# State space chunks of a hybrid decoder step: two products moved from GpSimd to VectorE, and the inter-chunk part added where the diagonal part is read from PSUM

## The chip, the cores and the metric

The kernel runs on one core of one Trainium2 chip. The metric is the device time of one execution in microseconds; lower is better. Engines are named as the profile names them: PE is TensorE (PEld its weight loads), DVE is VectorE, ACT is ScalarE, POOL is GpSimd, SP is SyncE, which issues most of the DMAs.

## The reference

One inference step of a hybrid decoder layer on 1024 prompt tokens and 8 x 4 sample tokens, width 1024, all in float32. The part that the change touches is the Mamba-2 mixer (16 heads of 64, two B/C groups, state 128), computed exactly in chunks of 128 tokens:

```python
CB = jnp.einsum('bclgn,bcsgn->bcgls', Cm, Bm)
y_diag = jnp.einsum('bcgls,bcgkls,bcsgkp->bclgkp', CB, Lmat, xdt)
states = jnp.einsum('bcsgn,bcsgk,bcsgkp->bcgkpn', Bm, decay_st, xdt)
def step(h, inp):
    st, dec = inp
    return h * dec[..., None, None] + st, h
y_off = jnp.einsum('bclgn,bcgkpn,bclgk->bclgkp', Cm, starts, jnp.exp(acs))
y = y_diag + y_off + xs * d_skip.astype(F32).reshape(G, K)[..., None]
```

Lmat is the lower triangle of exp of differences of the cumulative decays `acs`; `starts` are the states before each chunk. Beside it in the same layer stand a pooling mixer, a gated linear recurrence (LRU), an output projection, cross attention and a feed-forward part.

## The kernel before

Channels lie on partitions, tokens along the free dimension. A projection takes a strip of weights of 128 columns, in two halves of reduced precision (`whi`, `wlo`, made from `wraw` by ACT L123 and DVE L124), and streams the 1056 tokens in three pieces of 352 (`unit`, L147): 24 matmuls to a piece, into one of three PSUM tiles `mm`. For the x, B and C channels (`xbc_proj`, L516) ACT copies the piece out twice (L500, L501), DVE applies the convolution in three steps (L503, and L509 for the sample tokens), ACT takes the tanh (L530) and DVE finishes the SiLU (L531).

The state space chunks are a generator (`ssd`, L708) that is stepped from within the projections: `unit` calls `tick` twice, and a step that says `yield 4` goes on four ticks, that is two pieces, later. Each of the two groups g (eight heads each) goes through eight chunks. A chunk has two steps.

- `first` (L550): ACT turns the rows of decays that a DMA has spread over all partitions (tiles `seg`, two per chunk, L547) into exponentials, `ea` (L556) and `seg` (L558, L559). PE makes the scores C·B (`pcb`) and transposes B and x (L562, L569). DVE masks the scores into `cbm` (L564) and makes `xdt` (L571, from PSUM) and `xdd` (L573, from `xdt`). POOL multiplies both `seg` tiles by `cbm` (L575).
- `second` (L578): PE computes the inter-chunk part `po` (L584), the new state `pst` from `xdd` (L588) and the diagonal part `pdg` from `seg` and `xdt` (L596), one behind the other. DVE makes `yt` = `po` times `ea` (L585). POOL decays the state `hs` (L586, tile h in the profile) and DVE adds `pst` to it (L590). DVE adds x times the skip weight and `pdg` (L600, four times per chunk), and POOL adds `yt` to that (L602, four times).

Group 0 begins beside the projections of group 1's channels and runs on beside `pool` (L822), group 1 beside `pool` and `lru` (L760). While group 1 runs, the sample's state space steps (`ssd_sample`, L614) run too: POOL decays a state (L696), DVE adds to it (L700), ACT's queue issues its store (L701), and SP loads the next state into the same tile (L680). In `pool`, window sums go to and fro between DVE and POOL (L800, L812), ACT writes the result `ya` (L819). In `lru`, PE needs the convolved tile `xc` (L503) for its gates `pr` and `pi` (L722, L723).

The order of PE's and SP's instructions is that of the program text (L64). That of ACT, DVE and POOL is set by a scheduler in this part of the program. Every engine goes through its own list in order, and a DMA that ACT issues holds up what stands behind it on ACT until its data is there.

Of the kernel before, what the change touches and what calls it, by code (L numbers as in the profile page):

```python
# [12 lines left out]
OP = mybir.AluOpType  # L13
PSUM = bass.MemoryType.PSUM

P = 128
# [43 lines left out]
def hybrid_step(ctx, tc, xT, memT, consts_d, masks_d, wbd_d, poolw_d, spool_d, w_kv, w_xbc, w_dt, w_lg, w_pool, w_z, h0_d,  # L60
                w_out1, w_out2, w_q, kc_d, vc_d, w_o, w_gu, w_down,
                yT, ktT, vN, smallo, pssd, sssd):
    nc = tc.nc
# [11 lines left out]
    def nm(s):  # L75
        cnt[0] += 1
        return f"{s}{cnt[0]}"
# [30 lines left out]
    def smps(shape=(P, 512), name="sm"):  # L108
        return ps.tile(list(shape), F32, tag="sm", name=nm(name), bufs=sm_bufs)
# [58 lines left out]
    def cc(name, i=None, n=1):  # L168
        a, b = COFF[name]
        return cst[:, a:b] if i is None else cst[:, a + i:a + i + n]  # L170
# [247 lines left out]
    cd = sd.tile([P, 256], F32, name="cd")  # L418
# [95 lines left out]
    xbc = [None] * 12  # L514
# [18 lines left out]
    r8 = lambda t: t.rearrange("p (h q) -> p h q", h=8)  # L533

    def ssd_prompt(g):

        Bt, Ct = xbc[8 + g], xbc[10 + g]
        hs = sd.tile([P, 512], F32, tag=f"h{g}", name=nm("h"), bufs=1)
        tk = lambda c: slice(c * P, (c + 1) * P)
        h0 = lambda c: c * 16 + g * 8  # L540
        bc8 = lambda t, c: t[:, h0(c):h0(c) + 8][:, :, None].to_broadcast([P, 8, 64])

        def load(c):

            segs = [sd.tile([P, 4, P], F32, tag="seg", name=nm("seg"), bufs=4) for _ in range(2)]
            for q in range(2):
                nc.sync.dma_start(segs[q], acs_dram[None, h0(c) + 4 * q:h0(c) + 4 * q + 4, :].to_broadcast([P, 4, P]))  # L547
            return segs

        def first(c, segs):  # L550
            ea = sd.tile([P, 4, P], F32, tag="ea", name=nm("ea"), bufs=1)
            for q in range(2):
                seg, h = segs[q], h0(c) + 4 * q
                for i in range(2 if c else 0):
                    half = slice(i * 64, i * 64 + 64)
                    nc.scalar.activation(ea[half, 2 * q:2 * q + 2], seg[half].rearrange("p (j i) l -> p i j l", i=2)[:, i], AF.Exp)  # L556
                for j in range(4):
                    nc.scalar.activation(seg[:, j], seg[:, j], AF.Relu, scale=-1.0, bias=acs[:, h + j:h + j + 1])  # L558
                nc.scalar.activation(seg, seg, AF.Exp, scale=-1.0)  # L559
            pcb = smps(name="pcb")  # L560
            nc.tensor.matmul(pcb[:, :P], Bt[:, tk(c)], Ct[:, tk(c)], start=True, stop=True)
            nc.tensor.transpose(pcb[:, P:2 * P], Bt[:, tk(c)], ident)  # L562
            cbm = sd.tile([P, P], F32, tag="cbm", name=nm("cbm"), bufs=1)
            nc.vector.tensor_tensor(cbm, pcb[:, :P], tri, op=OP.mult)  # L564
            btok = sd.tile([P, P], F32, tag="btok", name=nm("btok"), bufs=1)
            nc.scalar.activation(btok, pcb[:, P:2 * P], AF.Copy)
            px = smps(name="px")
            for j in range(4):
                nc.tensor.transpose(px[:, j * P:(j + 1) * P], xbc[4 * g + j][:, tk(c)], ident)  # L569
            xdt = sd.tile([P, 512], F32, tag="xdt", name=nm("xdt"), bufs=2)  # L570
            nc.vector.tensor_tensor(r8(xdt), r8(px), bc8(dt, c), op=OP.mult)  # L571
            xdd = sd.tile([P, 512], F32, tag="xdd", name=nm("xdd"), bufs=1)
            nc.vector.tensor_tensor(r8(xdd), r8(xdt), bc8(dst, c), op=OP.mult)  # L573
            for seg in segs:
                nc.gpsimd.tensor_tensor(seg, seg, cbm[:, None, :].to_broadcast([P, 4, P]), op=OP.mult)  # L575
            return segs, ea, xdt, xdd, btok

        def second(c, segs, ea, xdt, xdd, btok):  # L578
            yt = sd.tile([P, 4, P], F32, tag="yt", name=nm("yt"), bufs=1)
            j4 = lambda t: t.rearrange("p (j l) -> p j l", j=4)  # L580
            if c:
                po = smps(name="po")
                for j in range(4):
                    nc.tensor.matmul(po[:, j * P:(j + 1) * P], hs[:, j * P:(j + 1) * P], Ct[:, tk(c)], start=True, stop=True)  # L584
                nc.vector.tensor_tensor(yt, j4(po), ea, op=OP.mult)  # L585
                nc.gpsimd.tensor_tensor(r8(hs), r8(hs), bc8(cd, c), op=OP.mult)  # L586
            pst = smps(name="pst")
            nc.tensor.matmul(pst, btok, xdd, start=True, stop=True)  # L588
            if c:
                nc.vector.tensor_tensor(hs, hs, pst, op=OP.add)  # L590
            else:
                nc.vector.tensor_copy(hs, pst)
            pdg = smps(name="pdg")
            for h in range(8):
                a, b = h % 2 * 64, h // 2 * P
                nc.tensor.matmul(pdg[a:a + 64, b:b + P], xdt[:, h * 64:(h + 1) * 64], segs[h // 4][:, h % 4, :], start=True, stop=True)  # L596
            for j in range(4):
                m = 4 * g + j
                x, y = xbc[m][:, tk(c)], pdg[:, j * P:(j + 1) * P]
                nc.vector.scalar_tensor_tensor(x, x, cc("dskip", m), y, op0=OP.mult, op1=OP.add)  # L600
                if c:
                    nc.gpsimd.tensor_tensor(x, x, yt[:, j, :], op=OP.add)  # L602

        segs = load(0)
        for c in range(NCK):
            a = first(c, segs)
            yield 4
            if c < NCK - 1:
                segs = load(c + 1)
            second(c, *a)  # L610
            yield 2
        nc.scalar.dma_start(pssd[:, g * 512:(g + 1) * 512], hs)
# [319 lines left out]
    with ExitStack() as at:  # L932
# [157 lines left out]
        def opairs(g):  # L1090
            r = []
            for m in range(4 * g, 4 * g + 4):
                hi, lo = slot(F32R, "oh"), slot2(F32R, "ol") if m == 4 else slot(F32R, "ol")
                for c in range(NCH):
                    nc.scalar.activation(hi[:, ch(c)], o[m][:, ch(c)], AF.Copy)
                    nc.vector.tensor_tensor(lo[:, ch(c)], o[m][:, ch(c)], hi[:, ch(c)].bitcast(F32), op=OP.subtract)
                r.append((hi, lo))
            return r
# [8 lines left out]
        op0 = opairs(0)  # L1107
# [17 lines left out]
        op1 = opairs(1)  # L1125
# [600 lines left out]
```

## Time and profile before

| | |
|---|---|
| time, median of 3 runs | 1786.41 us (1782.34 to 1787.78) |
| profiled execution: its own time | 1788.4 us |
| its span in the trace | 1786.6 us |
| PE busy | 1723.3 us, 96% |
| DVE busy | 1131.4 us, 63% |
| ACT busy | 811.7 us, 45% |
| POOL busy | 593.1 us, 33% |

The state space chunks lie between about 130 and 440 us of the span. A busy time is the sum of an engine's instructions; the table is an average over stages whose limits differ, so that the stages have to be read one by one. In a timeline row, the bracket at the end says how long the engine stood idle before the instruction, and what ended that.

### The profile page before, as it was taken

How to read it: one execution, taken by the hardware profiler on the slowest of the kernel's cores; microseconds unless marked ns; L12 is line 12 of the kernel's file. 1: busy time of each engine (PE TensorE's matmuls, PEld its weight loads, DVE VectorE, ACT ScalarE, POOL GpSimd, SP SyncE). 2: the span in 40 equal slices, each digit the busy share in tenths (PEclk: the TensorE clock that was granted, in tenths of full speed). 3: DMA queues.
4: the chain of work that ended last, by engine and by line, in shares of the span. 5: the costliest groups of instructions: out<-in, count | busy, mean ns of one | idle time of the engine just before them, and what ended most of it. 6: DMA issues, size and time to landing. Idle time of an engine off the chain costs nothing.

```text
span 1786.6 us, 31851 instructions
## 1 busy us (share of the span) xinstructions
PE 1723.3 (96%) x12307; PEld 1672.8 (94%) x12307; DVE 1131.4 (63%) x2045; ACT 811.7 (45%) x1650; POOL 593.1 (33%) x618
## 2 busy tenths in 40 slices
PE   8899999999999999999999989999999999899997
PEld 7799988888999999999999979999999999899896
DVE  4887877676844534455566479555555556786855
ACT  6546665678634313245565255222322224343344
POOL 2312446554232322212221243433343332211435
PEclk9999999999999999999999989999999999999998
DMA  9112123341320522233344230233322224543322
GB/s 344 68 48 68 65 70 92 107 145 57 125 83 31 210 84 84 79 131 121 116 140 165 90 144 32 85 115 107 105 100 91 96 90 170 199 164 112 118 72 98
DMA packets 106503, 197.51 MB, mean 111 GB/s; under 512 B 15344, under 2 KB 33392, under 8 KB 106352
## 3 DMA queue, kind: packets, MB, share of 16 engines
q1 hardware_dynamic: 94832, 173.54, 28.6%
q10 hardware_dynamic: 11520, 21.94, 3.3%
q8 instruction: 97, 1.59, 0.4%
q14 instruction: 54, 0.44, 0.1%
HBM read 151.54 MB, written 43.89 MB: 109 GB/s over the span
## 4 chain that ended last, share of the span: by engine, by line
PE 77%; DVE 10%; ACT 4%; issue 3%; POOL 3%; DMA 3%; SPq 0%; ACTq 0%; DVEq 0%; POOLq 0%
PE mm L152 12%; PE mm L154 12%; PE mm L153 12%; PE st L1325 10%; PE st L1326 10%; PE st L1327 10%; DVE cy L503 1%; PE poa L1082 1%; PE pss L1064 1%; ACT seg L558 1%; DVE xd L1371 1%; PE st L1453 1%; PE st L1455 1%; PE st L1454 1%; DMA xd<-hid_dram 1%
## 5 line engine op out<-in xcount | busy, mean ns | idle before, releaser
L152 PE MATMUL mm<-uh,whi 128*128 128x352 f32 x960 | 321.1, 334 | 1.1 <-ACT cy L501 1.1
L1325 PE MATMUL st<-x,whi 128*128 128x264 f32 x1120 | 318.9, 285 | 1.0 <-ACT tm L1505 0.5
L1326 PE MATMUL st<-x,whi 128*128 128x264 f32 x1120 | 318.1, 284 | 0.0
L1327 PE MATMUL st<-x,wlo 128*128 128x264 f32 x1120 | 318.0, 284 | 0.0
L154 PE MATMUL mm<-uh,wlo 128*128 128x352 f32 x960 | 311.1, 324 | 0.0
L153 PE MATMUL mm<-ul,whi 128*128 128x352 f32 x960 | 311.0, 324 | 0.0
L1325 PEld LDWEIGHTS st<-x,whi 128*128 128x128 f32 x1120 | 210.7, 188 | 1.6 <-ACT tm L1505 0.7
L1327 PEld LDWEIGHTS st<-x,wlo 128*128 128x128 f32 x1120 | 210.7, 188 | 0.0
L1326 PEld LDWEIGHTS st<-x,whi 128*128 128x128 f32 x1120 | 210.6, 188 | 0.0
L152 PEld LDWEIGHTS mm<-uh,whi 128*128 128x128 f32 x960 | 182.0, 190 | 5.7 <-issue 1.7
L153 PEld LDWEIGHTS mm<-ul,whi 128*128 128x128 f32 x960 | 182.5, 190 | 2.5
L154 PEld LDWEIGHTS mm<-uh,wlo 128*128 128x128 f32 x960 | 181.7, 189 | 0.0
L1325 PE MATMUL st<-xd,whi 128*128 128x264 f32 x504 | 144.6, 287 | 13.7 <-ACT w L1551 7.1
L1326 PE MATMUL st<-xd,whi 128*128 128x264 f32 x504 | 144.0, 286 | 0.0
L1327 PE MATMUL st<-xd,wlo 128*128 128x264 f32 x504 | 143.7, 285 | 0.0
L1258 ACT ACTIVATE whi<-as 128x512 fp32r<-128x512 f32 (+1 forms) x128 | 74.6, 584 | 139.5 <-PE st L1326 96.3
L1258 ACT ACTIVATE whi<-ar 128x512 fp32r<-128x512 f32 (+1 forms) x104 | 60.8, 588 | 150.4 <-PE st L1326 84.3
L123 ACT ACTIVATE whi<-wraw 128x512 fp32r<-128x512 f32 x128 | 77.5, 627 | 106.2 <-PE mm L153 80.1
L1243 POOL TENSOR_TENSOR as<-ar 128x512 f32<-128x512 f32 (+1 forms) x32 | 53.0, 1655 | 205.8 <-DVE wlo L1259 181.6
L124 DVE TENSOR_TENSOR wlo<-wraw,whi 128x512 fp32r<-128x512 f32 x128 | 96.0, 767 | 23.6 <-ACT whi L123 23.5
L1325 PEld LDWEIGHTS st<-xd,whi 128*128 128x128 f32 x504 | 95.6, 190 | 15.2 <-ACT w L1551 7.3
L957 POOL TENSOR_TENSOR kvlo<-kvraw,kvhi 128x512 fp32r<-128x512 f32 x32 | 41.4, 1295 | 163.2 <-ACT kvhi L956 125.3
(460 smaller groups left out, 4437.6 us busy)
## 6 DMA issues: line engine op xcount, KB each, us to landing
ar<-w_gu SPq DMA_DIRECT2D x88, 256.0 KB, 4.1
hid_dram<-tm SPq DMA_DIRECT2D x71, 264.0 KB, 2.1
xd<-hid_dram SPq DMA_DIRECT2D x63, 264.0 KB, 4.9
ar<-w_down SPq DMA_DIRECT2D x48, 192.0 KB, 3.2
h_dram<-h ACTq DMA_DIRECT2D x16, 528.0 KB, 3.0
h<-h_dram SPq DMA_DIRECT2D x16, 528.0 KB, 6.3
seg<-acs_dram SPq DMA_DIRECT2D x32, 256.0 KB, 3.9
wraw<-w_out SPq DMA_DIRECT2D x32, 256.0 KB, 3.6
```

The lines of the kernel that those rows point to most:

```text
L123: nc.scalar.activation(hi[:, a:b], raw, AF.Copy)
L124: nc.vector.tensor_tensor(lo[:, a:b], raw, hi[:, a:b].bitcast(F32), op=OP.subtract)
L152: nc.tensor.matmul(out, whi[:, a:b], xh[:, cols], start=k == 0, stop=False)
L153: nc.tensor.matmul(out, whi[:, a:b], xl[:, cols], start=False, stop=False)
L154: nc.tensor.matmul(out, wlo[:, a:b], xh[:, cols], start=False, stop=k == kk - 1)
L503: nc.vector.scalar_tensor_tensor(y[:, :n], raw[:, j:j + n], w[j], y[:, :n], op0=OP.mult, op1=OP.add)
L957: eng.tensor_tensor(lo, src, hi.bitcast(F32), op=OP.subtract)
L1243: nc.gpsimd.tensor_tensor(s1, a21, a22, op=OP.add)
L1258: nc.scalar.activation(hi[:, a], src, AF.Copy)
L1325: nc.tensor.matmul(out, whi[:, a:b], xh, start=begins and k == 0, stop=False, skip_group_check=True)
L1326: nc.tensor.matmul(out, whi[:, a:b], xl, start=False, stop=False, skip_group_check=True)
L1327: nc.tensor.matmul(out, wlo[:, a:b], xh, start=False, stop=k == kk - 1, skip_group_check=True)
```

## The change

Per chunk, the two products of decays and scores (L575) and the decay of the state (L586) go from POOL to DVE. The four additions of `yt` on POOL (L602 before) go away: in chunks after the first, DVE adds the whole `pdg` to `yt` in one instruction (L598 after), and the four instructions that add the skip part read the sum `yt` from SBUF where they read `pdg` from PSUM (L600 before, L602 after).

```diff
             for seg in segs:
-                nc.gpsimd.tensor_tensor(seg, seg, cbm[:, None, :].to_broadcast([P, 4, P]), op=OP.mult)
+                nc.vector.tensor_tensor(seg, seg, cbm[:, None, :].to_broadcast([P, 4, P]), op=OP.mult)
...
                 nc.vector.tensor_tensor(yt, j4(po), ea, op=OP.mult)
-                nc.gpsimd.tensor_tensor(r8(hs), r8(hs), bc8(cd, c), op=OP.mult)
+                nc.vector.tensor_tensor(r8(hs), r8(hs), bc8(cd, c), op=OP.mult)
...
+            if c:
+                nc.vector.tensor_tensor(yt, yt, j4(pdg), op=OP.add)
             for j in range(4):
                 m = 4 * g + j
-                x, y = xbc[m][:, tk(c)], pdg[:, j * P:(j + 1) * P]
-                nc.vector.scalar_tensor_tensor(x, x, cc("dskip", m), y, op0=OP.mult, op1=OP.add)
-                if c:
-                    nc.gpsimd.tensor_tensor(x, x, yt[:, j, :], op=OP.add)
+                x = xbc[m][:, tk(c)]
+                nc.vector.scalar_tensor_tensor(x, x, cc("dskip", m), yt[:, j] if c else pdg[:, j * P:(j + 1) * P],
+                                               op0=OP.mult, op1=OP.add)
```

POOL loses 102 instructions: 32 of L575, 14 of L586, 56 of L602. DVE gains 60: those 32 and 14, and 14 of the new L598. The lists of PE and SP stay as they were. Below L602 the line numbers of after are one higher.

On DVE, in group 0 beside the projections (`first` of a chunk), before:

```order
L531 SCALAR_TENSOR_TENSOR xbc_283_2034<-xbc_283_2034,cy_2127 128x352
L564 TENSOR_TENSOR cbm_2180<-pcb_2177,msk 128x128
L571 TENSOR_TENSOR xdt_2189<-px_2184,dt 128x512
L503 SCALAR_TENSOR_TENSOR cy_2195<-raw_2196,cst,cy_2195 128x320
L573 TENSOR_TENSOR xdd_2191<-xdt_2189,dst 128x512
```

And the same place after:

```order
L564 TENSOR_TENSOR cbm_2174<-pcb_2171,msk 128x128
L531 SCALAR_TENSOR_TENSOR xbc_283_2031<-xbc_283_2031,cy_2121 128x352
L571 TENSOR_TENSOR xdt_2183<-px_2178,dt 128x512
L575 TENSOR_TENSOR seg_2092<-seg_2092,cbm_2174 128x512
L573 TENSOR_TENSOR xdd_2185<-xdt_2183,dst 128x512
L575 TENSOR_TENSOR seg_2093<-seg_2093,cbm_2174 128x512
L503 SCALAR_TENSOR_TENSOR cy_2189<-raw_2190,cst,cy_2189 128x320
```

The two products stand on either side of `xdd`, and the convolution step that stood between `xdt` and `xdd` stands behind them.

On POOL, in the last pieces of `pool` (psb and pws are its window sums, h the sample's state), before:

```order
L791 COPY prs_3645<-praw_3642 128x8x4
L792 COPY outs<-praw_3642 128x15
L575 TENSOR_TENSOR seg_3516<-seg_3516,cbm_3627 128x512
L575 TENSOR_TENSOR seg_3517<-seg_3517,cbm_3627 128x512
L793 COPY outs<-prs_3645 128x120
L800 TENSOR_TENSOR pws_3653<-pws_3651 128x332
L812 TENSOR_TENSOR psb_3660<-prs_3645 128x8x18
L812 TENSOR_TENSOR psb_3662<-psb_3660 128x8x16
L812 TENSOR_TENSOR psb_3664<-psb_3662 128x8x12
L812 TENSOR_TENSOR psb_3666<-psb_3664 128x8x4
L800 TENSOR_TENSOR pws_3657<-pws_3655 128x320
L696 TENSOR_TENSOR h_3586<-h_3586,cd 128x512
```

And after:

```order
L792 COPY prs_3621<-praw_3618 128x8x4
L793 COPY outs<-praw_3618 128x15
L801 TENSOR_TENSOR pws_3629<-pws_3627 128x332
L794 COPY outs<-prs_3621 128x120
L813 TENSOR_TENSOR psb_3636<-prs_3621 128x8x18
L813 TENSOR_TENSOR psb_3638<-psb_3636 128x8x16
L813 TENSOR_TENSOR psb_3640<-psb_3638 128x8x12
L813 TENSOR_TENSOR psb_3642<-psb_3640 128x8x4
L801 TENSOR_TENSOR pws_3633<-pws_3631 128x320
L697 TENSOR_TENSOR h_3562<-h_3562,cd 128x512
```

The two products are gone from in front of the window sums.

On DVE, in `lru` beside group 1 (two pieces, `xc` of which the first is the one that PE's gates need first), before:

```order
L600 SCALAR_TENSOR_TENSOR xbc_339_2412<-xbc_339_2412,cst,pdg_4254 128x128
L600 SCALAR_TENSOR_TENSOR xbc_367_2601<-xbc_367_2601,cst,pdg_4254 128x128
L503 SCALAR_TENSOR_TENSOR xc_4206<-raw_4207,cst,xc_4206 128x352
L695 COPY yof_3585<-pof_4294 128x4x4
L503 SCALAR_TENSOR_TENSOR xc_4206<-raw_4207,cst,xc_4206 128x352
L503 SCALAR_TENSOR_TENSOR xc_4273<-raw_4274,cst,xc_4273 128x352
L503 SCALAR_TENSOR_TENSOR xc_4206<-raw_4207,cst,xc_4206 128x352
```

And after:

```order
L590 TENSOR_TENSOR h_3109<-h_3109,pst_4221 128x512
L598 TENSOR_TENSOR yt_4213<-yt_4213,pdg_4224 128x512
L503 SCALAR_TENSOR_TENSOR xc_4176<-raw_4177,cst,xc_4176 128x352
L602 SCALAR_TENSOR_TENSOR xbc_283_2031<-xbc_283_2031,cst,yt_4213 128x128
L503 SCALAR_TENSOR_TENSOR xc_4176<-raw_4177,cst,xc_4176 128x352
L602 SCALAR_TENSOR_TENSOR xbc_311_2217<-xbc_311_2217,cst,yt_4213 128x128
L503 SCALAR_TENSOR_TENSOR xc_4176<-raw_4177,cst,xc_4176 128x352
```

The three convolution steps of the first piece stood behind all four of L600, with one of the second piece between them; now the third stands behind two of them, and the second piece comes later.

## Rows read from the trace of the kernel before

**Rows 1.** Stages: busy us of PE, PEld, DVE, ACT, POOL; granted clock; DMA share, GB/s

```profile
130.00:270.00 140.00, 137.31 (x915) 130.10 (x914) 112.64 (x219) 88.31 (x221) 55.64 (x112) 1.00 0.21 68
270.00:330.00 60.00, 60.00 (x421) 53.27 (x419) 43.97 (x85) 29.26 (x75) 38.94 (x58) 1.00 0.31 96
330.00:445.00 115.00, 106.97 (x677) 96.35 (x676) 83.50 (x173) 90.95 (x171) 56.55 (x81) 0.99 0.30 104
```

**Rows 2.** Waits of PE from 130 to 445 us: sum, times, longest (us)

```profile
PE px L569 <- ACT ya L819: 3.3, 1, 3.3
PE pst L588 <- DVE xdd L573: 2.6, 2, 1.3
PE pr L722 <- issue: 1.8, 1, 1.8
PE pst L588 <- ACT btok L566: 1.7, 2, 1.3
PE pr L722 <- PE mm L154: 0.9, 1, 0.9
PE pdg L596 <- POOL seg L575: 0.3, 2, 0.2
```

**Rows 3.** Groups by line and shape, 130 to 445 us: busy us, mean ns, idle before

```profile
L573 DVE TENSOR_TENSOR xdd<-xdt,dst 128x512 f32<-128x512 f32 x16 | 20.3, 1268 | 0.1
L600 DVE SCALAR_TENSOR_TENSOR xbc<-xbc,cst,pdg 128x128 f32<-128x128 f32 x64 | 18.0, 336 | 0.7 <-PE pdg L596 0.6
L590 DVE TENSOR_TENSOR h<-h,pst 128x512 f32<-128x512 f32 x14 | 9.5, 676 | 2.2 <-PE pst L588 1.8 <-POOL h L586 0.4
...
L575 POOL TENSOR_TENSOR seg<-seg,cbm 128x512 f32<-128x512 f32 x32 | 45.0, 1423 | 11.4 <-DVE cbm L564 8.4 <-ACT seg L559 2.7
L602 POOL TENSOR_TENSOR xbc<-xbc,yt 128x128 f32<-128x128 f32 x56 | 28.5, 537 | 21.5 <-DVE xbc L600 21.5
L586 POOL TENSOR_TENSOR h<-h,cd 128x512 f32<-128x512 f32 x14 | 15.0, 1073 | 1.5 <-PE po L584 1.5
```

**Rows 4.** Timeline, group 0 beside the projections: start, duration, engine, line, operation

```profile
187.50 1.77 DVE L573 TENSOR_TENSOR xdd<-xdt,dst 128x512 f32<-128x512 f32 x1
192.21 1.02 PE L588 MATMUL pst<-xdd,btok 128*128 128x512 f32 x2
204.40 1.78 DVE L573 TENSOR_TENSOR xdd<-xdt,dst 128x512 f32<-128x512 f32 x1
207.57 1.02 PE L588 MATMUL pst<-xdd,btok 128*128 128x512 f32 x2
219.74 2.81 POOL L575 TENSOR_TENSOR seg<-seg,cbm 128x512 f32<-128x512 f32 x2
219.96 1.44 DVE L503 SCALAR_TENSOR_TENSOR cy<-raw,cst,cy 128x320 f32<-128x320 f32 x1 [0.81 <-ACT cy L501]
```

**Rows 5.** Timeline and chain before the longest wait of PE; last, clock of one microsecond

```profile
319.35 2.97 POOL L575 TENSOR_TENSOR seg<-seg,cbm 128x512 f32<-128x512 f32 x2
323.27 0.71 DVE L800 TENSOR_TENSOR pws<-pws 128x328 f32<-128x328 f32 x1 [2.10 <-POOL pws L800]
328.62 0.67 DVE L700 TENSOR_TENSOR h<-h,psts 128x512 f32<-128x512 f32 x1
329.77 0.56 ACT L819 ACTIVATE ya<-pp,cst 128x352 f32<-128x352 f32 x1 [7.02 <-DVE h L700]
332.49 4.08 DMA seg<-acs_dram
336.65 0.85 ACT L556 ACTIVATE ea<-seg 64x256 f32<-64x256 f32 x2 [4.74 <-DMA seg<-acs_dram]
340.69 1.11 PE L569 MATMUL px<-msk,xbc 128*128 128x128 f32 x4 [3.33 <-ACT ya L819]
...
341.00:342.00 1.00, 1.00 (x6) 1.00 (x5) 0.16 (x1) 0.48 (x2) 0.00 (x0) 0.50 0.48 177
```

**Rows 6.** Timeline before the wait of the LRU gates

```profile
379.60 3.14 DVE L503 SCALAR_TENSOR_TENSOR xc<-raw,cst,xc 128x352 f32<-128x352 f32 x4
```

## Prediction

> **What bounds the kernel now.** I began with the engines by stage. From 130 to 270 us, where group 0's chunks run beside the projections, PE is busy 137.31 of 140 us; from 330 to 445 us, beside the LRU, 106.97 of 115 [rows 1]. The reader is to see two things there. PE sets the end, so work that is taken from POOL is worth nothing by itself: only time in which PE stands still can be won. And DVE, which is to take the work over, is already busy for 112.64 of the 140 us, 80%.
>
> The second view is PE's waits. From 130 to 445 us they come to 3.3 + 2.6 + 1.8 + 1.7 + 0.9 + 0.3 = 10.6 us [rows 2], 0.6% of the span. That, and what the clock loses after a long wait, is about all there is to win. POOL itself is named for 0.3 us of it. So the question is whether POOL stands behind the waits that bear other engines' names.
>
> The third view is the groups by line, for how DVE and POOL get in each other's way. L573 (`xdd`, both inputs in SBUF) takes 1268 ns on average, L590 of the same size (one input in PSUM) 676 [rows 3]. The timeline shows what the difference is: while POOL runs its two L575 (219.74 to 222.55), a convolution step of DVE takes 1.44 us, and `xdd`, always next in line, 1.77 [rows 4]. L600, which reads PSUM, shows a mean of 336 ns [rows 3]. So each chunk costs DVE about 1.77 - 0.68 = 1.1 us on `xdd`, and about 0.8 us on the step before it (1.44 against roughly 0.6 for a shape that is smaller than L590's by a third).
>
> **The change part by part.**
>
> *DVE's work.* Per chunk DVE gets two L575, one L586 and one L598. No row of before shows them there. L575 and L586 are bounded below by L590's 0.68 us, and above by L573's blocked 1.27; L598 is L590's shape, 0.68. I take 0.68 for all four, since the POOL work that would block them is mostly what goes away: 45.0 + 28.5 + 15.0 = 88.5 us [rows 3] of the 55.64 + 38.94 + 56.55 = 151 that POOL has in the three stages [rows 1]. That is 2.7 us added per chunk. Removed is what POOL's L575 costs DVE now, 1.9 us, and some tenths for L586. Net: +0.4 to +0.8 us per chunk; with all four at the upper end, +2.5.
>
> *The four L600* now have both inputs in SBUF. [...] By the rows I price this so: some 60 us of POOL work stay in the 315 us, a fifth of the time; if a fifth of the four L600 of a chunk lost 0.6 us each (as L573 does on average), it would be 0.5 us per chunk. It is inside the bounds that follow.
>
> *Wait one, `pst` for `xdd`, 2.6 us* [rows 2]. `xdd` comes every 204.40 - 187.50 = 16.90 us, but PE asks for it every 207.57 - 192.21 = 15.36 us [rows 4]. So DVE and ACT, each waiting for the other in turn, are the slower loop; PE's lead of 2.9 us (192.21 - 189.27) melts by 1.5 us per chunk, and the last two chunks of this stage wait 1.3 us each. In the new order `xdd` stands behind `xdt` and one product, 0.7 us, where 1.44 us of convolution stood, and takes 0.7 in place of 1.77: it ends 1.8 us sooner. Of the loop's 16.90 us DVE is busy 80%, 13.6, and waits 3.3. With 0.5 more work it is 14.1 of work; if all waits stayed it would be 17.4 (the lead melts by 2.0 per chunk and `pst` waits some 2 us more in all, less the 1.8), if none stayed, PE's 15.36 would rule. I take about 15.8, because L586 and L598 fall where DVE waits now for ACT's run of exponentials, and because the scheduler puts ACT's copy (L501) in front of a tanh for which it waited. Then the lead is never used up: **-2.6 us**, between -2.6 and +2.
>
> *Wait two, `px` for `ya`, 3.3 us* [rows 2]. Followed back [rows 5]: `px` waits for a PSUM tile that ACT's `ya` frees; ACT is late because it stood 4.74 us for the `seg` rows; these were issued at 332.49 by SP, behind a reload that waits for a store; that store waited for DVE's L700, which ended at 329.3, and held ACT too (7.02 us). And DVE reached L700 late because it stood 2.10 us for a window sum of POOL, which was queued behind POOL's two L575 (319.35 to 322.3); further window sums, queued likewise, held it again. With the L575 gone from POOL the sums are done about 3 us sooner. DVE pays 1.4 us for its own L575, but in time in which it waited, and its `xdd` there takes 0.7 less. I reckon L700 3 us sooner, the whole chain of store, reload and `seg` behind it likewise, and `px` 3 us sooner against a wait of 3.3. [...] Together **-4.8 us**; the lower end is nothing (the chain is late for its DMAs alone), the upper end these 4.8.
>
> *Wait three, `pr`, 1.8 us "issue".* PE needs the third L503 of a piece; four of them took 3.14 us, 0.78 each, one of another piece in between [rows 6]. In the new order the third stands behind two skip additions fewer and nothing of the other piece: 3 x 0.6 + 2 x 0.34 = 2.5 us from its first, where it took about 3.4. Ahead of it stand L586 and L598, 1.4 us more; but the POOL products that blocked DVE here are gone (about 1.1), as is DVE's wait for POOL's L586. I take -1.4 here and -0.3 for `seg`, which POOL delivers late here and in a later chunk: **-1.7 us**, between -2.1 and +1.
>
> *Wait four, `pst` for `btok`, 1.7, and the second `pr`, 0.9* [rows 2]: `btok` is late on ACT, which stood for DVE's gate products behind the scan; no POOL work stands in that. Unchanged: **0**, from -0.9 to +1.
>
> That POOL has less to do is worth nothing elsewhere: only 0.3 us of PE's waits name it [rows 2]. SP's and PE's lists are unchanged, and from 445 us on the program is the same, so what PE wins until then should stay won.
>
> **The sum.** -2.6 - 4.8 - 1.7 = -9.1 us, 0.5%. Against the profiled execution, whose own time was 1788.4 us, this is 1779.3; against the median of the runs, 1786.41, which lies 2 us lower, it is 1777.3. I forecast **1778 us**.
>
> **The rivals.**
>
> *The chain of wait two keeps its length.* From the end of L700 to `px` lie 11 us, most of them DMAs (the `seg` rows alone 4.08 us from issue to landing [rows 5]) and ACT's exponentials; none of that gets shorter. If PE, being 2.6 us earlier through wait one, gets there earlier by as much as the chain does, PE waits on, and the clock falls as before. Then only waits one and three are won: -4.3, 1782 us. For it: the chain is long and PE's own gain works against it. Against it: the chain's start hangs on `praw` and `px`, which PE itself delivers, so that PE's gain moves both.
>
> *DVE becomes the bound, and it gets slower.* If `xdd` at 1.77 us is not POOL's doing, or POOL's remaining work blocks the new instructions just as much, DVE gets 2.7 us per chunk and loses none: 13.6 + 2.7 = 16.3 of work and 3.3 - 1 of waits, a loop of some 18.6 us. The lead that PE has a chunk before the first of [rows 4], 2.9 + 1.5 = 4.4 us, then melts by 3.2 per chunk and is gone in the second; over five chunks PE waits some 5 x 3.2 - 4.4 = 12 us in place of 2.6, at `pst`. With some microseconds for `pr` in the LRU stage, less 2 for POOL's window sums: +10, 1796 us. It decides from a loop of 16.9 us on, the present one. For it: DVE at 80%. Against it: the gap between L573 and L590, and that L573 takes 0.69 wherever no L575 runs beside it (its 16 run from 674 to 1786 ns; the mean is in [rows 3]).
>
> *It does nothing that matters.* PE's loop hides all of it, or small new waits return what was won: 1784 to 1788.
>
> **How the numbers follow.** My forecast, with all of one and three and most of two, 0.58. The chain that keeps its length, 0.20. Nothing that matters, 0.12. DVE as the bound, 0.10. What a measurement of this kernel can tell from no change is 0.3%, 5.4 us: faster means below 1781. The forecast's case is below that nearly always (0.56 of 0.58), and the kept chain at times (0.04 of 0.20): faster 0.60, same 0.30, slower 0.10. The range goes from 1772 (all 10.6 us of waits, 1.5 of clock and some tenths of each wait that the view doesn't count) to 1787; what is left out is DVE as the bound, and a little on either side.
>
> **What would show it.** In the profile of the changed kernel: L573 at a mean near 0.7 us, the distance of two `xdd` in group 0 between 15.4 and 16.2 us, no `pst` waiting for `xdd`; no wait of `px` near 335 us and no clock of 0.50 there; `pr` waiting under 0.5 us near 378; DVE some 10 us busier, POOL some 88 us less. I am wrong if `xdd` comes every 17 us or more, if L602 of after takes well over 0.34 us, or if PE's wait for `ya` is still there.

## The result, and the profile after

The changed kernel takes **1775.5 us**, the median of 6 runs (1773.72 to 1776.31); the kernel before took 1786.72 beside it. The ratio is 0.9946, with a 95% interval of 0.9933 to 0.9958. That is 11.2 us less, or 0.5%, well beyond what can be told from no change. Measured again with other kernels on another chip it was 1776.48, ratio 0.9943 [0.9931, 0.9956]. The forecast was 1778, in a range from 1772 to 1787. The profiled execution took 1776.31 us, with a span of 1774.5 (before: 1786.6).

I read the same views as before. Engines over the whole span, from the page:

```profile
PE 1718.7 (97%) x12307; PEld 1668.6 (94%) x12307; DVE 1137.5 (64%) x2105; ACT 813.5 (46%) x1650; POOL 515.2 (29%) x516
```

The three stages, with the columns of [rows 1]:

```profile
130.00:270.00 140.00, 140.00 (x937) 133.07 (x936) 116.30 (x255) 93.78 (x231) 22.47 (x70) 1.00 0.23 71
270.00:330.00 60.00, 60.00 (x420) 53.27 (x419) 47.10 (x99) 26.98 (x67) 23.81 (x40) 1.00 0.34 109
330.00:445.00 115.00, 112.36 (x733) 101.43 (x733) 93.45 (x206) 94.55 (x176) 27.35 (x44) 1.00 0.30 99
```

PE's waits from 130 to 445 us, as in [rows 2]:

```profile
PE pst L588 <- ACT btok L566: 1.3, 1, 1.3
PE pr L723 <- PE mm L154: 1.1, 2, 0.7
```

In group 0's stage PE now stands at 140.00 of 140.00 us, and the granted clock is 1.00 in all three. Six rows of waits with 10.6 us have become two with 2.4. `px` for `ya`, `pst` for `xdd`, `pr` for "issue" and `pdg` for POOL's `seg` are gone. POOL's share of these stages fell from 151 to 73.6 us.

The groups by line, as in [rows 3] (from L602 on, a line's number is one higher than before):

```profile
L503 DVE SCALAR_TENSOR_TENSOR cy<-raw,cst,cy 128x352 f32<-128x352 f32 (+1 forms) x75 | 42.6, 569 | 4.0 <-ACT cy L501 2.7 <-POOL outs L510 0.5
...
L575 DVE TENSOR_TENSOR seg<-seg,cbm 128x512 f32<-128x512 f32 x32 | 22.9, 721 | 3.4 <-ACT seg L559 3.3
...
L602 DVE SCALAR_TENSOR_TENSOR xbc<-xbc,cst,yt 128x128 f32<-128x128 f32 x56 | 17.1, 361 | 0.2
...
L573 DVE TENSOR_TENSOR xdd<-xdt,dst 128x512 f32<-128x512 f32 x16 | 11.2, 703 | 0.1
...
L586 DVE TENSOR_TENSOR h<-h,cd 128x512 f32<-128x512 f32 x14 | 10.1, 722 | 0.0
...
L598 DVE TENSOR_TENSOR yt<-yt,pdg 128x512 f32<-128x512 f32 x14 | 9.5, 680 | 0.3 <-PE pdg L596 0.3
```

`xdd` fell from 1268 to 703 ns without any edit to it. The three groups new on DVE cost 680 to 722 ns each, 42.5 us together. Yet DVE is only 6 us busier over the span, since what it did already got shorter: `xdd` by 9.1 us, the convolution steps (L503) by 9.0, the rest in smaller pieces.

The timeline of DVE, three `xdd` in a row in group 0, and that of PE, two `pst`, as in [rows 4]:

```profile
201.23 0.69 DVE L573 TENSOR_TENSOR xdd<-xdt,dst 128x512 f32<-128x512 f32 x1
216.96 0.69 DVE L573 TENSOR_TENSOR xdd<-xdt,dst 128x512 f32<-128x512 f32 x1
232.67 0.68 DVE L573 TENSOR_TENSOR xdd<-xdt,dst 128x512 f32<-128x512 f32 x1
```

```profile
207.41 1.02 PE L588 MATMUL pst<-xdd,btok 128*128 128x512 f32 x2
222.77 1.02 PE L588 MATMUL pst<-xdd,btok 128*128 128x512 f32 x2
```

The distance of two `xdd` is 15.72 us where it was 16.90; that of two `pst` is 15.36 as before. PE's lead melts by 0.36 us per chunk and no longer by 1.5, and the group is over before it is used up.

The chain that led to the wait of `px` [rows 5], in the changed kernel's timeline:

```profile
318.16 0.83 DVE L815 SCALAR_TENSOR_TENSOR pl<-psb,prs 128x32 f32<-128x32 f32 x1 [0.60 <-POOL psb L813]
...
321.65 0.67 DVE L701 TENSOR_TENSOR h<-h,psts 128x512 f32<-128x512 f32 x1
322.80 0.56 ACT L820 ACTIVATE ya<-pp,cst 128x352 f32<-128x352 f32 x1 [3.66 <-DVE h L701]
...
329.34 0.85 ACT L556 ACTIVATE ea<-seg 64x256 f32<-64x256 f32 x2 [4.58 <-DMA seg<-acs_dram]
...
332.79 0.56 ACT L820 ACTIVATE ya<-pp,cst 128x352 f32<-128x352 f32 x1
```

For the window sums of this piece DVE now stands 0.60 us in all, where it stood 2.10 [rows 5] and then another 1.07 us. The add into `h` (L700, now L701) comes 6.97 us sooner (328.62 to 321.65), of which 3.6 is PE's own gain up to there; the last `ya` of this chain 7.3 us sooner (340.08 to 332.79). PE no longer waits for it.

**Where the time went, by one landmark.** A single profiled time says little about a few microseconds: the second profile of the changed kernel had a span of 1771.3 us, 3.2 less than the first, with the same waits up to 445 us. The starts of the `po` matmuls (L584) say more, since up to the last of them the two profiles of the changed kernel agree within 0.05 us per stretch. These are the first and last `po` of group 0, and the first, the third and the last of group 1. Before:

```profile
175.96 1.05 PE L584 MATMUL po<-xbc,h 128*128 128x128 f32 x8
...
272.72 1.05 PE L584 MATMUL po<-xbc,h 128*128 128x128 f32 x8
308.12 1.05 PE L584 MATMUL po<-xbc,h 128*128 128x128 f32 x8
...
352.66 1.05 PE L584 MATMUL po<-xbc,h 128*128 128x128 f32 x8
...
432.96 1.05 PE L584 MATMUL po<-xbc,h 128*128 128x128 f32 x8
```

After:

```profile
175.80 1.05 PE L584 MATMUL po<-xbc,h 128*128 128x128 f32 x8
...
269.12 1.05 PE L584 MATMUL po<-xbc,h 128*128 128x128 f32 x8
304.52 1.05 PE L584 MATMUL po<-xbc,h 128*128 128x128 f32 x8
...
344.34 1.05 PE L584 MATMUL po<-xbc,h 128*128 128x128 f32 x8
...
421.94 1.05 PE L584 MATMUL po<-xbc,h 128*128 128x128 f32 x8
```

Group 0 went from 96.76 to 93.32 us (-3.44: wait one), the stretch with the wait of `px` from 44.54 to 39.82 (-4.72: wait two), the rest of group 1 from 80.30 to 77.60 (-2.70: waits three and four); between the groups lie 35.40 in both. Together that is -10.86 us. In the last stretch, -2.34 fall between `po` of 371.46 and 394.40 (wait three) and -0.36 behind 412.08 (wait four).

### The profile page after: what moved, and what is told of

Its sections match the earlier page's. It is cut to its first block, busy times and chain, and to the rows that moved or that the text cites. A ratio compares the mean times of both kernels' runs of the same rounds, so it can differ in the third digit from the quotient of the medians.

```text
span 1774.5 us, 31790 instructions
## 1 busy us (share of the span) xinstructions
PE 1718.7 (97%) x12307; PEld 1668.6 (94%) x12307; DVE 1137.5 (64%) x2105; ACT 813.5 (46%) x1650; POOL 515.2 (29%) x516
## 4 chain that ended last, share of the span: by engine, by line
PE 87%; DVE 6%; DMA 2%; ACT 2%; issue 2%; POOL 1%; SPq 0%; ACTq 0%; DVEq 0%; POOLq 0%
PE mm L152 14%; PE mm L154 14%; PE mm L153 14%; PE st L1326 10%; PE st L1327 10%; PE st L1328 10%; PE pss L1065 1%; PE poa L1083 1%; DVE x L330 1%; PE st L1454 1%; PE pdg L596 1%; PE st L1455 1%; PE st L1456 1%; DVE xd L1372 1%; PE psa L1014 1%
## 5 line engine op out<-in xcount | busy, mean ns | idle before, releaser
L124 DVE TENSOR_TENSOR wlo<-wraw,whi 128x512 fp32r<-128x512 f32 x128 | 92.2, 740 | 21.9 <-ACT whi L123 21.8
L1328 PEld LDWEIGHTS st<-xd,wlo 128*128 128x128 f32 x504 | 95.7, 190 | 0.0
```

What stands on the lines that cost most here:

```text
L124: nc.vector.tensor_tensor(lo[:, a:b], raw, hi[:, a:b].bitcast(F32), op=OP.subtract)
L1328: nc.tensor.matmul(out, wlo[:, a:b], xh, start=False, stop=k == kk - 1, skip_group_check=True)
```

## The experiments

My theory was that POOL's segment products (L575) make waits one and two: wait one because POOL's work holds up DVE's instructions with two SBUF inputs (`xdd` takes 1268 ns, L590 of the same size with one input in PSUM 676 [rows 3]), wait two mostly because POOL's window sums, for which DVE waits, stand behind these products in POOL's own list. The rivals: the order or number of instructions does it; the other two edits do it; the chain of wait two keeps its length. The table has all kernels, by the same landmark: what each of the three stretches gained or lost against before, their sum (with the stretch between the groups), and the time of the kernel less that of before in the same set of runs. The first three columns are single profiles. The last is a difference of medians, and the ratio's interval is some ±0.0013, or 2.3 us. In two kernels in which group 0 is as it was (one chunk, and group 1 alone) its stretch still differs from before by 0.12 and 0.20 us, so tenths in the table mean little.

| kernel | group 0 | to the third `po` of group 1 | rest | sum | time | ratio |
|---|---|---|---|---|---|---|
| changed kernel | -3.44 | -4.72 | -2.70 | -10.86 | -11.2 | 0.9946 |
| changed kernel again | -3.44 | -4.76 | -2.71 | -10.91 | -9.2 | 0.9943 |
| segment products alone | -3.44 | -4.72 | -1.54 | -9.70 | -6.6 | 0.9960 |
| decay alone | +0.09 | -0.70 | -1.63 | -2.24 | -1.9 | 0.9986 |
| merge alone | +0.59 | +1.16 | -0.58 | +1.17 | +0.2 | 0.9998 |
| changed, products back on POOL | -0.18 | -0.27 | -1.27 | -1.72 | -1.7 | 0.9996 |
| `xdd` from PSUM | -3.34 | -2.53 | +0.33 | -5.52 | -7.6 | 0.9959 |
| changed, idle products on POOL | -0.79 | +3.09 | -1.22 | +1.08 | 0.0 | 0.9998 |
| products moved, one chunk | +0.12 | -1.23 | -0.01 | -1.12 | -2.8 | 0.9983 |
| products moved, group 0 | -3.44 | -1.90 | +0.49 | -4.85 | -3.5 | 0.9980 |
| products moved, group 1 | +0.20 | -4.99 | -1.45 | -6.24 | -5.2 | 0.9971 |
| changed, `xdd` from PSUM | -3.34 | -4.92 | -2.87 | -11.12 | -8.7 | 0.9948 |
| changed, `btok` on DVE | -3.44 | -4.10 | +2.04 | -5.50 | -4.3 | 0.9975 |

**The parts one by one.** The segment products alone, in the kernel before:

```diff
-                nc.gpsimd.tensor_tensor(seg, seg, cbm[:, None, :].to_broadcast([P, 4, P]), op=OP.mult)
+                nc.vector.tensor_tensor(seg, seg, cbm[:, None, :].to_broadcast([P, 4, P]), op=OP.mult)
```

> Before, with only the two products of decays and scores (L575) moved to DVE. Theory (POOL's L575 is what costs: it holds up DVE's instructions with two SBUF inputs, and POOL's own queue): most of the gain of the whole change, -8 to -11 us, 1776 to 1779; no PE wait for xdd, none for ya near 340 us, L573 near 0.7 us. Rival (the merge of the additions, 28.5 us of POOL work and 56 instructions, is what counts): 1785 to 1788.

Measured: 1779.06 us against 1785.66, 6.6 us less where I expected 8 to 11; by the landmarks it is 9.70 of the whole change's 10.86. No wait for `xdd` or `ya` is left, `xdd` takes 698 ns, and the first two stretches gain to the hundredth what the whole change gains. `pr` still waits 1.6 us for "issue".

The state decay alone:

```diff
-                nc.gpsimd.tensor_tensor(r8(hs), r8(hs), bc8(cd, c), op=OP.mult)
+                nc.vector.tensor_tensor(r8(hs), r8(hs), bc8(cd, c), op=OP.mult)
```

> Before, with only the decay of the state (L586) moved to DVE. Theory: nothing that can be told from no change, 1785 to 1788; PE's waits for xdd and ya stay. Rival (any POOL work that leaves helps in proportion, 15 of 88.5 us): -2 us.

Measured: 1783.74, ratio 0.9986 [0.9976, 0.9996]. That is below the 1785 to 1788 that I expected and at the rival's -2 us, though not by the rival's reason: the merge, tested next, takes almost twice as much work from POOL and wins nothing. `xdd` stays at 1269 ns and its wait at 2.8 us, that of `px` at 2.5. But `pr`'s wait for "issue" is gone. So this one edit ends wait three, and the segment products don't.

The merge alone:

```diff
+            if c:
+                nc.vector.tensor_tensor(yt, yt, j4(pdg), op=OP.add)
...
-                x, y = xbc[m][:, tk(c)], pdg[:, j * P:(j + 1) * P]
-                nc.vector.scalar_tensor_tensor(x, x, cc("dskip", m), y, op0=OP.mult, op1=OP.add)
-                if c:
-                    nc.gpsimd.tensor_tensor(x, x, yt[:, j, :], op=OP.add)
+                x = xbc[m][:, tk(c)]
+                nc.vector.scalar_tensor_tensor(x, x, cc("dskip", m), yt[:, j] if c else pdg[:, j * P:(j + 1) * P],
+                                               op0=OP.mult, op1=OP.add)
```

> Before, with only the merge: yt plus pdg in one DVE instruction, the four POOL additions gone. Theory: within 2 us of before, 1784 to 1788; L573 stays near 1.27 us, the waits for xdd (2.6) and ya (3.3) stay. Rival (merge is what counts): 1776 to 1779.

Measured: 1785.85, ratio 0.9998 [0.9985, 1.0011]. Waits one and two stand at 3.3 and 3.2 us. That 28.5 us of POOL work [rows 3] are gone is worth nothing that shows in the time. In the second stretch PE even lost 1.16 us: its granted clock was 0.89 from 320 to 350 us (before: 0.94). (Both other edits without the merge were not tried.)

The changed kernel with the products back on POOL (the first diff, reversed):

> After, with only L575 put back on POOL. Theory: most of the gain is gone, 1783 to 1788; L573 back near 1.27 us, xdd again every 16.9 us, the waits for xdd and ya back. Rival (merge and decay carry the gain): 1775 to 1778.

Measured: 1783.99, ratio 0.9996 [0.9983, 1.0008]; `xdd` 1268 ns, PE waits 2.5 us for it and 2.9 for `ya`. The two runs with the segment products moved alone and back agree: they carry the first two waits, all but 0.2 to 0.3 us of each.

**Is it the meeting of two SBUF inputs with POOL?** In the kernel before, `xdd` was made from `px` in PSUM times a product formed once, with POOL's work as it was:

```diff
+    ddt = sd.tile([P, 144], F32, name="ddt")
...
+        nc.vector.tensor_tensor(ddt, dst, dt, op=OP.mult)
...
-            nc.vector.tensor_tensor(r8(xdd), r8(xdt), bc8(dst, c), op=OP.mult)
+            nc.vector.tensor_tensor(r8(xdd), r8(px), bc8(ddt, c), op=OP.mult)
```

> Before, with POOL's L575 left where they are, but xdd (the same line, one lower) made from the PSUM tile px times a product of dt and decay that is formed once, so that it has one input in PSUM. Theory (POOL holds up DVE instructions with two SBUF inputs, not those that read PSUM): xdd takes 0.68 us on average in place of 1.27 although POOL's L575 runs beside it; xdd is done about 1.1 us sooner, the pst waits for xdd (2.6 us) go or halve; px's wait for ya stays: 1782 to 1785. Rival (xdd is slow for a reason of its own, its broadcast or its place): its mean stays above 1.1 us and the time at 1786.

Measured: 1779.01 us against 1786.61, a larger gain than I expected (1782 to 1785). Its groups by line (numbers two higher than before):

```profile
L577 POOL TENSOR_TENSOR seg<-seg,cbm 128x512 f32<-128x512 f32 x32 | 43.3, 1367 | 11.9 <-DVE cbm L566 8.4 <-ACT seg L561 3.2
...
L575 DVE TENSOR_TENSOR xdd<-px,ddt 128x512 f32<-128x512 f32 x16 | 10.9, 682 | 0.0
```

With POOL's 32 products still beside it, `xdd` takes 682 ns and not 1268: one input in PSUM is enough, so its place, its size and its broadcast are not what made it slow. How POOL's work makes the instruction longer, no trace shows. Wait one is gone (-3.34). `px` still waits 2.2 us for `ya` and `pr` its 1.8. What I had not foreseen is that the clock stays at 1.00 from 320 to 350 us, so that the second stretch gains 2.53 us where the wait is only 1.1 us shorter. The landmarks leave 2 of the 7.6 us to the rest of the kernel.

The other way round, POOL was given two products per chunk that nobody needs, in the changed kernel:

```diff
                 nc.vector.tensor_tensor(seg, seg, cbm[:, None, :].to_broadcast([P, 4, P]), op=OP.mult)
+                side = sd.tile([P, 4, P], F32, tag="side", name=nm("side"), bufs=1)
+                nc.gpsimd.tensor_tensor(side, cbm[:, None, :].to_broadcast([P, 4, P]), cbm[:, None, :].to_broadcast([P, 4, P]), op=OP.mult)
```

> After, and beside it POOL makes two products of the size of L575 per chunk whose result nobody uses (cbm times cbm into a tile of its own). Theory: it is POOL's being busy that costs; L573 and L575 on DVE go to 1.1 us and more where they meet it, xdd comes every 16.9 us or later, window sums of POOL are late again: 1784 to 1795. Rival (the new order of DVE's and ACT's lists is what wins): 1775 to 1777.

Measured: 1786.59 us, ratio 0.9998 [0.9989, 1.0007]. The whole gain is gone, though nobody waits for the result of these products. Its groups by line, and its longest wait of PE:

```profile
L577 POOL TENSOR_TENSOR side<-cbm 128x512 f32<-128x512 f32 x32 | 38.9, 1215 | 40.2 <-DVE cbm L564 39.5
L575 DVE TENSOR_TENSOR seg<-seg,cbm 128x512 f32<-128x512 f32 x32 | 27.5, 865 | 2.5 <-ACT seg L559 2.4
...
L573 DVE TENSOR_TENSOR xdd<-xdt,dst 128x512 f32<-128x512 f32 x16 | 15.8, 989 | 0.1
```

```profile
PE pcb L561 <- ACT ya L822: 5.2, 1, 5.2
```

On average `xdd` is back at 989 ns. In the middle of group 0, though, it does not meet the idle products; there the first L575 does:

```profile
222.05 1.22 DVE L575 TENSOR_TENSOR seg<-seg,cbm 128x512 f32<-128x512 f32 x1
223.19 0.69 DVE L573 TENSOR_TENSOR xdd<-xdt,dst 128x512 f32<-128x512 f32 x1
...
239.47 0.69 DVE L573 TENSOR_TENSOR xdd<-xdt,dst 128x512 f32<-128x512 f32 x1
```

DVE's list in these chunks is that of the changed kernel, instruction for instruction, and DVE stands no longer for anyone. One instruction takes 1.22 us where it took 0.68, and the distance of two `xdd` is 16.28 us where it was 15.72: the 0.54 of that one instruction, to a few hundredths. Here neither an order nor a wait for POOL can be the reason. I had expected 16.9 us or more, which was too much.

The wait for `ya`, now of `pcb`, which stands just ahead of `px`, is longer than it was, and PE's granted clock is 0.89 from 320 to 350 us. The link of the chain that the prediction called late, the add into `h`, stands in DVE's timeline about where it stood before (328.62), 7.3 us behind its place in the changed kernel, of which 3.2 are PE's own lateness:

```profile
328.95 0.67 DVE L703 TENSOR_TENSOR h<-h,psts 128x512 f32<-128x512 f32 x1
```

For this chain the run does not tell the two ways apart: the idle products stand in POOL's list ahead of window sums, and DVE's own instructions beside them are longer too.

**Does the chain of wait two keep its length?** First the products went to DVE in one chunk only, the one ahead of the wait:

```diff
-                nc.gpsimd.tensor_tensor(seg, seg, cbm[:, None, :].to_broadcast([P, 4, P]), op=OP.mult)
+                (nc.vector if (g, c) == (1, 2) else nc.gpsimd).tensor_tensor(seg, seg, cbm[:, None, :].to_broadcast([P, 4, P]), op=OP.mult)
```

> Before, with L575 on DVE in one chunk alone, the third of group 1, whose two products stand on POOL from 319 to 322 us in front of the window sums. Theory: the wait of px for ya (3.3 us) and the clock of 0.50 behind it go, the waits for xdd stay: -4 to -5 us, 1781 to 1783. Rival (that chain is late by its DMAs): wait stays over 2.5 us, 1786.

Measured: 1783.79, ratio 0.9983 [0.9974, 0.9992]. `px` still waits 2.0 us, less than the rival's 2.5 and not gone as in my theory, whose 1781 to 1783 the time misses as well. The clock fell all the same (0.94 from 320 to 350 us, as before). Then in group 0 only (`nc.gpsimd if g else nc.vector` on the same line), so that PE gains ahead of the chain and nothing in it changes:

> Before, with L575 on DVE in group 0 alone. Theory: xdd every 15.4 to 15.9 us, no pst waiting for xdd; px's wait for ya and the clock dip stay: -3 to -4 us, 1782 to 1784. Rival (kept chain: PE's being earlier lengthens the wait for ya by as much): 1786.

Measured: 1783.11, ratio 0.9980 [0.9972, 0.9989]. Wait one is gone to the hundredth (-3.44), and `px` waits 2.9 us; the clock's fall, which I expected to stay, did not come. And in group 1 only (`nc.vector if g else nc.gpsimd`):

> The kernel before, with the segment products (L575) on DVE in group 1's chunks only; in group 0 they stay on POOL. If the wait of px for ya is made by POOL in group 1's own chunks (and one chunk was merely too few of them), the wait of 3.3 us is gone, the clock stays at 1.00 from 320 to 350 us, and pr's 1.8 us go too, while pst still waits about 2.6 us for xdd in group 0: 4.8 + 1.7 less than before, about 1780. If the lateness is handed over from group 0, px still waits about 2 us, as with one chunk alone: about 1783.

Measured: 1780.47, ratio 0.9971 [0.9958, 0.9984], as the first theory had it. `pst` waits 2.9 us for `xdd` in group 0; there is no wait for `ya`, and the stretch gains 4.99 us. One number of its expectation failed: `pr` still waits 1.5 us. The timelines of the one chunk and of group 1 tell why one chunk was not enough. One chunk:

```profile
325.98 0.67 DVE L700 TENSOR_TENSOR h<-h,psts 128x512 f32<-128x512 f32 x1
330.40 0.90 SPq L547 DMA_DIRECT2D seg<-acs_dram  x2
334.72 0.85 ACT L556 ACTIVATE ea<-seg 64x256 f32<-64x256 f32 x2 [5.64 <-DMA seg<-acs_dram]
338.76 0.82 PE L569 MATMUL px<-msk,xbc 128*128 128x128 f32 x4 [1.97 <-ACT ya L819]
```

Group 1:

```profile
325.53 0.67 DVE L700 TENSOR_TENSOR h<-h,psts 128x512 f32<-128x512 f32 x1
329.22 0.90 SPq L547 DMA_DIRECT2D seg<-acs_dram  x2
332.91 0.85 ACT L556 ACTIVATE ea<-seg 64x256 f32<-64x256 f32 x2 [4.28 <-DMA seg<-acs_dram]
```

L700 starts 2.64 and 3.09 us sooner than before (328.62). In the first of these profiles, however, PE is ahead by 0.56 us at the `po` before it (326.55 against 327.11), in the second by 0.05. Against PE, L700 gains 2.08 and 3.04 us: the prediction's "3 us sooner" holds with all of group 1, and two thirds of it with the chunk that the prediction named. The rest of the chain does not keep its length: from the start of L700 to `ea` it was 8.03 us before (336.65 - 328.62), 8.74 with one chunk and 7.38 with group 1; the differences lie in the store and reload ahead of the issue (3.87, 4.42, 3.69) and in the rows' landing (4.16, 4.32, 3.69). The changed kernel has 7.69 (329.34 - 321.65). So this part gave another 0.65 in one kernel and took 0.71 in the other. With one chunk that makes 2.08 - 0.71 = 1.37 us, and the wait went from 3.33 to 1.97; with group 1 it makes 3.69, more than the wait. Why the DMAs differ by 1.4 us was not settled.

**Is there a better version?** The changed kernel with `xdd` from PSUM (the diff above):

> The changed kernel, with xdd formed from px in PSUM times a product of decay and dt that is made once, in place of from xdt in SBUF. If the changed kernel has really won all that POOL took from xdd, nothing is left to win there (xdd at 0.70 us goes to 0.68): 1774 to 1776.5, as the changed kernel. If what remains of POOL's work still blocks xdd where PE waits, up to another 1 us is won.

Measured: 1777.0, ratio 0.9948 [0.9935, 0.9961], against 1776.48 for the changed kernel beside it, half a microsecond above what I expected. Nothing is left to win at `xdd`.

The changed kernel with `btok`, the last wait of PE, copied by DVE:

```diff
-            nc.scalar.activation(btok, pcb[:, P:2 * P], AF.Copy)
+            nc.vector.tensor_copy(btok, pcb[:, P:2 * P])
```

> The changed kernel, with btok (L566) copied out of PSUM by DVE in place of ACT. The 1.3 us that pst still waits for btok are ACT's: if nothing takes their place, they are gone and the kernel takes about 1774, 1.5 us less than the changed kernel. If DVE's extra copy of some 0.25 us per chunk, ahead of xdt and xdd, makes a new wait of pst for xdd or of pr, it is 1775 to 1777.

Measured: 1781.39, some 5 us slower than the changed kernel, where I had expected at most 1.5. No wait for `btok` is left, but PE has a new one:

```profile
PE pdg L596 <- DVE seg L575: 4.6, 2, 2.5
```

The first of its two costs the time. In the timelines of ACT, DVE and PE ahead of it:

```profile
364.09 1.28 ACT L756 ACT_TABLE_LOAD   x1
...
365.86 1.28 ACT L559 ACT_TABLE_LOAD   x1
367.16 0.63 ACT L559 ACTIVATE seg<-seg 128x512 f32<-128x512 f32 x1
367.82 0.69 DVE L575 TENSOR_TENSOR seg<-seg,cbm 128x512 f32<-128x512 f32 x1 [0.36 <-ACT seg L559]
368.56 0.66 PE L596 MATMUL pdg<-seg,xdt 128*64 128x128 f32 x8 [2.09 <-DVE seg L575]
```

In the changed kernel the same exponential stands ahead of L756, without a table load of its own:

```profile
363.29 0.61 ACT L559 ACTIVATE seg<-seg 128x512 f32<-128x512 f32 x1
363.92 1.28 ACT L756 ACT_TABLE_LOAD   x1
```

With `btok` gone from its list, ACT takes the function of the LRU's gate (L756) first, and two table loads of 1.28 us now stand between the tile's preparation and its exponential. PE waits 2.09 us, and then its granted clock is 0.51 from 370 to 374 us and 0.63 from 374 to 378. From this chunk's `po` to the next it is 25.38 us, in the changed kernel 20.60: nearly the whole loss. So the trace points to the order of ACT's list, not to the copy's own 0.28 us on DVE; no run put the order back to test it. (The profiled execution took 1773.66 us, less than the median; up to 445 us its landmarks show the loss all the same.)

The last kernel was the changed one as it is:

> The changed kernel as it is, on the same chip, so that the two variants of it have something to be compared with: 1775.5, between 1773.5 and 1776.5. Both theories expect the same of it.

Measured: 1776.48 us (1773.09 to 1777.63). No kernel tried is better than it.

## Why the prediction was right, point by point

**PE sets the end, and POOL stands behind waits that bear other names.** Right. Removing 28.5 us of POOL's work by the merge is worth nothing, while the 45.0 us of the segment products are worth most of the gain, with no row of PE's waits naming POOL for more than 0.3 us. The chain of work that ended last is made of PE for 77% of the span before, and for 87% after.

**DVE's work.** The three products were taken at 0.68 us; they measure 0.68 to 0.72. That L602, with both inputs in SBUF, would be held up by POOL as `xdd` was, had been priced at 0.5 us per chunk of four; it is 4 x (0.361 - 0.336) = 0.1. DVE became 6 us busier, where some 10 were said; POOL fell by 78, where 88 were said.

**Wait one** was put at -2.6 us, with the loop at 15.8 us; the loop is 15.72, and the stretch gains 3.44. The cause is settled from both sides: moving the products in group 0 alone gains exactly this, and so, to 0.1 us, does taking one of `xdd`'s inputs from PSUM (3.34); idle products make the loop longer again (16.28 us). The size was off by 0.8, because I took the gain to be the sum of the waits that the view lists. The two chunks with waits of 1.3 us were 1.50 and 1.54 us longer from `po` to `po`, and the chunk before them, with no wait in the list, 0.40.

**Wait two** was put at -4.8, of 3.3 wait and 1.5 clock; it is -4.72. The 1.5 was my estimate, and no run shows it by itself. What the runs show in its place is, first, the granted clock of the kernel before: behind the stand of 3.33 us it was 0.50 from 341 to 342 us [rows 5], and then

```profile
342.00:343.00 1.00, 1.00 (x5) 1.00 (x4) 0.53 (x1) 1.00 (x4) 0.08 (x1) 0.50 0.71 266
343.00:344.00 1.00, 1.00 (x5) 1.00 (x5) 0.23 (x1) 1.00 (x3) 1.00 (x4) 0.56 0.00 0
344.00:345.00 1.00, 1.00 (x8) 1.00 (x7) 1.00 (x2) 1.00 (x3) 0.70 (x2) 1.00 0.65 211
```

Against a clock of 1.00 these three microseconds fall short by 0.50 + 0.50 + 0.44 = 1.44 us, by estimate. Second, the clock's part has a witness: with the products moved in group 0 only, `px` still stands for 2.88 us, but PE's granted clock is 1.00 from 320 to 350 us (before: 0.94), and the stretch is 1.90 us shorter. Less the 0.45 that the wait itself is shorter, that leaves 1.45 for the clock's fall. The way through POOL's list is borne out in its main link: DVE stands 0.60 us for window sums in this piece where it stood 3.17, and L700 comes 3.0 us sooner against PE when group 1's products leave POOL. That the rest of the chain would move along by as much was wrong; it gave or took up to 0.7 us. In the changed kernel it gave 0.34, so that chain and L700 together gained 3.7 us against a wait of 3.3. That all of the 4.8 came rests on these 0.4 us and is partly luck.

**Wait three** was put at -1.7 and measures -2.34 in its piece. The step that named the products that block DVE and DVE's wait for POOL's L586 together was half right: L586 on DVE alone ends the "issue" wait (it is gone there, and 1.6 us remain with the segment products alone). How the two together make 2.70, and not the 1.54 + 1.63 that they make alone, was not followed up. **Wait four** was put at nothing, and gave 0.36.

**From 445 us on** I said that PE's gain stays won. It stays only on average. At 455 us PE is 11.06 us ahead, at 600 us 9.25, at the end 12.1. One place is plain: the same wait (`pb` for `nr`, 2.1 us before and 2.3 after) was followed by a granted clock of 1.00 in the kernel before and of 0.83 in the changed one. The windows before and after:

```profile
580.00:590.00 10.00, 7.93 (x53) 7.72 (x52) 6.41 (x16) 5.70 (x10) 3.38 (x5) 1.00 0.89 330
```

```profile
570.00:580.00 10.00, 7.68 (x42) 7.47 (x41) 5.41 (x11) 4.77 (x8) 3.02 (x3) 0.83 0.87 320
```

So the 1778 came out 2.5 us too high because waits one and three were undersized by 1.5 us together and wait four by 0.4, and because I took 1778 where the sum, counted from the median, gave 1777.3. That these add up so well is partly luck: behind 445 us PE's lead moves by more than 2 us, and two profiles of one kernel differ by more.

**The rivals.** The chain that keeps its length does so when only PE's own gain acts on it (group 0 alone: `px` waits 2.9 of 3.3 us), and in part with one chunk; with group 1's products moved the wait is gone. So what spoke against this rival was not PE's gain, as the prediction had it, but the products in group 1 alone. DVE as the bound: `xdd` at 1.77 us was POOL's doing, and the loop got shorter, not longer. With idle POOL work beside it the loop grew to 16.28 us, still under the 16.90 of before.

## What to carry to other kernels

A helper engine that is not the bound one can cost the bound engine time with hardly a wait that names it: here POOL, busy for 33% of the span, is named for 0.3 us of PE's waits [rows 2], and moving its segment products alone gained 9.70 us by the landmarks. What gave it away was a comparison of means, 1268 ns for an instruction that reads two SBUF tiles and 676 for one of the same size that reads PSUM [rows 3], and POOL's products beside the first in the timeline [rows 4]. The same comparison can be made in any trace; what it is worth there, only a run of that kernel tells. Here two edits brought the blocked instruction back: with the POOL work on DVE it took 0.70 us, with one of its inputs in PSUM 0.68, and the first made DVE only 6 us busier. Count a gain by a landmark of the bound engine, stage by stage, not by one profile's end, and read the lists of all engines again after each edit: here a moved copy of 0.28 us came with another order on the engine that it left, and new waits of 4.6 us.

## What the runs showed that I had not expected

- 32 POOL products that nobody waits for, 38.9 us of a unit that was 29% busy, undo the whole gain of 11 us.
- POOL's products differ in length too: the 32 of L575 run from 1264 to 1747 ns in the kernel before, with a mean of 1423 [rows 3]. With `xdd` from PSUM the mean is 1367, with `xdd` from SBUF and the products of group 1 moved it is 1477 for the 16 left on POOL, so how much of it is `xdd`'s doing is open.
- After a stand of 3.33 us PE's clock fell to 0.50 [rows 5]; after one of 2.88 us at the same wait (group 0 alone) it stayed at 1.00 from 320 to 350 us, and after one of 1.97 us there (one chunk) it was 0.94 in the same stretch; after the one of 2.32 us near 575 us it was 0.83 from 570 to 580 us, after the one of 2.07 us in the kernel before 1.00 from 580 to 590. The length of the stand alone doesn't decide it.
- The changed kernel's two profiles, equal to 0.05 us per stretch up to 445 us, lie 4.1 us apart from 1060 to 1480 us, and 3.2 at the end. The waits near 1030 us differ, and PE's granted clock from 1050 to 1060 us, 0.71 in one and 0.86 in the other; why was not looked into.
